# mLSTM and GLA values in one 512-column projection: one pass of the weights over five PSUM banks, ahead of the mLSTM

## The chip, the cores and the metric

The program runs on one NeuronCore of a Trainium2 chip. The metric is the device time of one execution in microseconds (us); lower is better. TensorE (PE) does the matmuls, VectorE (DVE), ScalarE (ACT) and GpSimd (POOL) the elementwise work, SyncE (SP) issues the DMAs.

## What is computed

Two layers of a diffusion backbone on 640 tokens of width 1024: 128 context tokens (tile 0) and 512 latent tokens (tiles 1 to 4). Cut to what the change touches:

```python
(mq, mk, mv, mo, mg, gq, gk, gv, gg, ga, acq, ackv, akr) = split(h @ w_in)   # one input projection
hf, state = mlstm_scan(q, k, v, gates...)        # v from mv, 4 heads x 64 = 256 columns
hb, state = mlstm_scan(flipped ...)
m_out = head_norm(hf + flip(hb)) * sigmoid(mo)
of, Sf = gla_scan(q, k, v, lg_f, S0)             # v from gv, 4 heads x 64 = 256 columns
ob, Sb = gla_scan(flipped ...)
g_out = head_norm(of + flip(ob)) * silu(gg)
a_out = mla_attention(...)                       # from acq, ackv, akr
out = concat(m_out, g_out, a_out) @ w_out
```

After this mixer each layer has a LayerNorm, a SwiGLU and a second LayerNorm. The four 256-column parts mv, gv, mo and gg have the same input `h` and the same form of product.

## The kernel before

Activations stand transposed in SBUF as `hT`: for each of 8 slices of the model width a 128-row tile, with columns for the tokens (groups of 256 and 384). All large products are made from a high and a low part of each factor, so that one product takes three matmuls (`mm3`, line 62: h·wh, h·wl, l·wh). Weights come by DMA into `raw` (4 buffers) and `wsplit` (line 117) makes the two parts: ACT writes `wh`, DVE or POOL writes `wl` (3 buffers each).

The mixer (line 323) has two ways of projecting. `a_tile` (line 349) holds the weights still and streams tokens, so that its result has features on partitions. `b_tiles` (line 361) holds 128 tokens still and streams 256 columns of weights: for each of the 5 token tiles, 8 slices × 3 matmuls of 128x256 into one PSUM bank `accB`, then an eviction. `b_quarter` (line 377) runs all its tiles. Its four uses in a layer, 120 matmuls each, are:

- quarter 0 (mv), line 406, ahead of the mLSTM, evicted by ACT into `v1`;
- quarter 1 (gv), line 661, in the program text behind the mLSTM and the GLA's q and k projections, evicted by ACT into `gv`;
- quarters 2 (mo) and 3 (gg), lines 704 and 858, which become gates.

The mLSTM (lines 409 to 580) first turns gate rows into scans on DVE (`rowF`, `rowBC`, `rowI`), transposes them on PE (`tokT`), then updates the states `C` position by position (`U` on PE, `kw` and `C` on DVE), and last runs five token tiles, each with `Mb`, `qk` and `hnum` on PE, `Dt` on ACT, POOL and DVE. The GLA first makes gates (`z` on PE; `zb`, `ze` on DVE and ACT) and chunk ends (`ep` and `khT` on PE; `lgl`, `kx`, `qh` on DVE), lines 594 to 634; then state updates (`U2`, shown as `U`, with `S` on DVE) and, for each token tile, `gla_levels`, `gla_scores` and `gla_rows` (lines 731 to 808: `Xq` on DVE, `Xk` on POOL, `lv`, `lw` and `go` on PE). In layer 0 the conditioning weights are used beside all this: `ada` (line 168) loads 1 MB at a time into the one buffer `araw4` and multiplies it by 4 matmuls; `weave(n)` advances it by n such steps.

Order of the work: the text above is the program order only. A scheduler sets each engine's order by readiness and program order, so independent projections fill PE between dependent steps. Engines take their own instructions strictly in that order. PSUM has 8 banks: in the mixer ring `a` has 2, `q` 2, and `b` 3 in layer 0 (with 1 for `ada`) or 4 in layer 1.

Of the kernel before, what the change touches and what calls it, by code (L numbers as in the profile page):

```python
# [6 lines left out]
F32 = mybir.dt.float32  # L7
F32R = mybir.dt.float32r
AF = mybir.ActivationFunctionType
# [5 lines left out]
L = 2  # L15
D = 1024
NT = 5
# [14 lines left out]
def tcol(t):  # L32
    return (0, t * 128) if t < 2 else (1, (t - 2) * 128)


def build(nc, tc, I, O, dbg=None, layers=L, stop=None):
    V, S, P, T = nc.vector, nc.scalar, nc.gpsimd, nc.tensor
# [7 lines left out]
    def act(out, in_, f, **kw):  # L45
        return S.activation(out=out, in_=in_, func=f, **kw)  # L46
# [70 lines left out]
    def wsplit(src, n=1024, own=None, e=V):  # L117
        r = raw()
        dma(r[:, :n] if len(src.shape) == 2 else
            r[:, :n].rearrange("p (a b) -> p a b", a=src.shape[1]), src)  # L120
        p, tag, bufs = own or (wp, "w", SPL)
        h = p.tile([128, 1024], F32R, tag=tag + "h", bufs=bufs, name="wh")
        l = p.tile([128, 1024], F32R, tag=tag + "l", bufs=bufs, name="wl")
        act(h[:, :n], r[:, :n], AF.Copy)
        tt(l[:, :n], r[:, :n], h[:, :n].bitcast(F32), SUB, e=e)
        return h, l
# [196 lines left out]
    def mixer(l, hT, adas, pm0, ws=None):  # L323
# [11 lines left out]
        g0 = g0s.enter_context(pool(f"glas{l}"))  # L335
# [25 lines left out]
        def b_tiles(q, evac, wv=0):  # L361
            ws = []
            for u in range(2):
                weave(wv)
                ws.append(wsplit(I["w_inB"][l, q, u]))
            for t in range(NT):
                g, o = tcol(t)
                h, lo = hT[g]
                acc = pa("accB")
                for k in range(8):  # L370
                    wh, wl = ws[k // 4]
                    c = slice((k % 4) * 256, (k % 4) * 256 + 256)
                    mm3(acc[:, :256], (h[:, k, o:o + 128], lo[:, k, o:o + 128]), (wh[:, c], wl[:, c]), k == 0, k == 7)
                evac(acc[:, :256], t)
                yield

        def b_quarter(q, evac, wv=0):
            for _ in b_tiles(q, evac, wv):
                pass
# [5 lines left out]
        v1 = mp.tile([128, NT, 4, 65], F32, name="v1")  # L385
# [7 lines left out]
        else:  # L393
            todo = [(g, f) for g in range(2) for f in first]
            for part in (todo[:5], todo[5:]):
                accs = [pt("aabbb"[i], "acc") for i in range(len(part))]
                for kk in range(4):
                    for acc, (g, ((src, M), (wh, wl), dst)) in zip(accs, part):
                        h, lo = hT[g]
                        for k in range(2 * kk, 2 * kk + 2):  # L400
                            c = slice(k * M, k * M + M)
# [1 line left out]
                for acc, (g, ((src, M), w, dst)) in zip(accs, part):  # L403
                    act(dst[:, GO[g]:GO[g] + GN[g]], acc[:M, :GN[g]], AF.Copy)

        b_quarter(0, lambda acc, t: act(v1[:, t, :, 0:64], acc.rearrange("p (h v) -> p h v", h=4), AF.Copy))


        R = [64, NT, 128]
# [34 lines left out]
        mo = mp.tile([64, NT], F32, name="mo")  # L444
# [60 lines left out]
        for j in range(0, 4):  # L505
            for d in range(2):
                t = pos2tile(d, j)
# [18 lines left out]
        for t in range(NT):  # L526
            c = slice(t * 128, (t + 1) * 128)
# [53 lines left out]
        m1.close()  # L581


        gv = g0.tile([128, NT, 256], F32, name="gv")
        qh = [pp.tile([128, 2, 128], F32, name=f"qh{t}") for t in range(NT)]
        kh = [pp.tile([128, 2, 128], F32, name=f"kh{t}") for t in range(NT)]
        zb = [g0.tile([128, 256], F32, name=f"zb{t}") for t in range(NT)]
# [70 lines left out]
        a_tile(I["w_inA"][l, 6], 128, evs(kg), wv=3)  # L658
        for t in ORD:
            gla_gates(t)  # L660
        b_quarter(1, lambda acc, t: act(gv[:, t, :], acc, AF.Copy), wv=3)
        kxs = {}
        for i, t in enumerate(ORD):
            kxs[i] = gla_ends(t)
# [771 lines left out]
def layout(x):  # L1436
    f = np.float32
    o = _consts()
    o["xp"] = x["x_prompt"].reshape(128, D)
    o["xs"] = x["x_sample"].reshape(512, D)  # L1440
    o["cT"] = np.stack([x["c_ctx"].reshape(8, 128).T, x["c"].reshape(8, 128).T], 2)
    o["w_ada"], o["b_ada"] = x["w_ada"], x["b_ada"]
    w = x["w_in"]
    sp = np.cumsum((128, 128, 256, 256, 16, 128, 128, 256, 256, 32, 256, 128, 32))[:-1]
    mq, mk, mv, mo, mg, gq, gk, gv, gg, ga, acq, ackv, akr = np.split(w, sp, axis=2)
    sw = np.concatenate([np.arange(8, 16), np.arange(0, 8), np.arange(24, 32), np.arange(16, 24)])

    def mt(a):
        return a.reshape(L, 8, 128, a.shape[2]).transpose(0, 2, 1, 3).reshape(L, 128, -1)
    o["w_inA"] = np.stack([mt(a) for a in (acq[..., :128], acq[..., 128:], ackv, mq, mk, gq, gk)], 1)  # L1450
    o["w_inM"] = mt(np.concatenate([akr, akr[..., sw], ga, mg], 2))

    def halves(a):
        n = a.shape[1] // 256
        return a.reshape(L, n, 2, 128, 2, 512).transpose(0, 4, 1, 3, 2, 5).reshape(L, 2, n, 128, 1024)
    o["w_inB"] = np.stack([a.reshape(L, 2, 4, 128, 256).transpose(0, 1, 3, 2, 4).reshape(L, 2, 128, 1024)
                           for a in (mv, gv, mo, gg)], 1)
    gb = np.zeros((L, 64, 2), f)
    b = x["m_gate_b"]
    gb[:, 0:4, 0], gb[:, 0:4, 1] = b[:, 0:4], b[:, 4:8]  # L1460
    gb[:, 32:36, 0], gb[:, 32:36, 1] = b[:, 8:12], b[:, 12:16]
    o["gbias"] = gb
    o["gn"] = np.concatenate([x["m_norm_g"], x["g_norm_g"]], 1)
    w2 = np.zeros((L, 32, 256), f)
    w2[:, 0:16, 0:128] = x["g_w2"][:, 0]
    w2[:, 16:32, 128:256] = x["g_w2"][:, 1]
    o["g_w2"] = w2
    o["g_b2"] = x["g_b2"].reshape(L, 256)
    o["agn"] = np.stack([x["a_q_norm_g"][:, :128], x["a_q_norm_g"][:, 128:], x["a_kv_norm_g"]], 2)
    uq = x["a_w_uq"].reshape(L, 2, 128, 8, 96)  # L1470
    nope, rope = uq[..., :64].reshape(L, 2, 128, 512), uq[..., 64:]
    o["w_uq"] = np.concatenate([nope, rope.reshape(L, 2, 128, 256), rope[..., sw].reshape(L, 2, 128, 256)], 3)
    ukv = x["a_w_ukv"].reshape(L, 128, 8, 128)
    o["w_ukv"] = np.concatenate([ukv[..., :64].reshape(L, 128, 512), ukv[..., 64:].reshape(L, 128, 512)], 2)
    o["ckvT"] = x["cache_mla_ckv"][0].transpose(0, 2, 1)
    o["krT"] = x["cache_mla_krope"][0].transpose(0, 2, 1)
    o["w_out"] = halves(x["w_out"])
    ln = np.stack([x["ln1_g"], x["ln1_b"], x["ln2_g"], x["ln2_b"]], 1)
    o["ln_rows"] = ln
    o["ln_fm"] = ln.reshape(L, 4, 8, 128).transpose(0, 3, 1, 2)  # L1480
    for n in ("gate", "up"):
        o["w_" + n] = x["w_ffn_" + n].reshape(L, 8, 128, NM, 128).transpose(0, 3, 2, 1, 4).reshape(L, NM, 128, 1024)
    o["w_down"] = x["w_ffn_down"].reshape(L, NM, 128, 2, 512).transpose(0, 3, 1, 2, 4)
    ci = np.zeros((L, 2, 4, 32, 4, 65), f)
    si = np.zeros((L, 2, 4, 32, 4, 64), f)
    for h in range(4):
        ci[:, :, h, :, h, :64] = x["state_mlstm_C"][0][:, :, h]
        ci[:, :, h, :, h, 64] = x["state_mlstm_n"][0][:, :, h]
        si[:, :, h, :, h] = x["state_gla_S"][0][:, :, h]
    o["cinit"] = ci.reshape(L, 2, 128, 260)  # L1490
    o["sinit"] = si.reshape(L, 2, 128, 256)
    m0 = np.zeros((L, 64, 1), f)
    m0[:, 0:4, 0] = x["state_mlstm_m"][0][:, 0]
    m0[:, 32:36, 0] = x["state_mlstm_m"][0][:, 1]
    o["m0"] = m0
    return {k: np.ascontiguousarray(v) for k, v in o.items()}
# [29 lines left out]
```

## Time and profile before

| what | value |
|---|---|
| three runs | 1853.81, 1857.25, 1860.08 us (median 1857.25) |
| the profiled execution | 1855.06 us, of which its span is 1853.3 us |
| mean granted TensorE clock | 0.968 of full speed |
| busy share of the span | PE 94%, PE weight loads 83%, DVE 58%, ACT 37%, POOL 19% |
| layer 0 mixer, from the first `accB` to the first `racc` (attention's q) | 60.6 to 285.9 us |
| layer 1 mixer, the same stretch | 992.8 to 1187.9 us |

Matmuls overlap in the pipeline: the duration of one is longer than the step to the next, so costs are taken from start to start. A granted clock of 1.00 in a stretch is 2.4 GHz, 0.50 is 1.2 GHz.

### The profile page before, as it was taken

Reading aid. Unit: us, or ns where it says so; the run is one execution under the profiler, and the core shown is the slowest. Engines: PE = TensorE matmul, PEld = TensorE weight load, DVE = VectorE, ACT = ScalarE, POOL = GpSimd, SP = SyncE. Lnnn points to the kernel's source line nnn. Section 1 sums busy time; section 2 is a strip of 40 time slices with the busy share of each in tenths; the row PEclk is TensorE's granted clock in tenths of the full one; section 3 lists DMA queues with packets and bytes.
Section 4 is the critical chain, followed back from the end, with each engine's and each line's share of the span. In section 5 each row is a group of like instructions: output and inputs, shape, how many; then the busy total and the mean of one; then the engine's idle time right before and its main releaser. Section 6 shows DMA issues by size and latency. Waiting matters only on the chain.

```text
span 1853.3 us, 28755 instructions
## 1 busy us (share of the span) xinstructions
PE 1745.0 (94%) x11360; PEld 1535.3 (83%) x11360; DVE 1072.2 (58%) x1996; ACT 685.2 (37%) x1418; POOL 343.7 (19%) x286
## 2 busy tenths in 40 slices
PE   7989888989999999999989999899999999999996
PEld 4867777768999899899868887776789989989995
DVE  3545588646588757564476667776475234233237
ACT  4335357643422122122243455576262212222221
POOL 0011435321330000000031136334026000000003
PEclk9989999999999999999998899899999999999998
DMA  9654322023246445342223223211412222213211
GB/s 317 231 141 163 111 59 62 18 107 114 93 159 207 139 138 163 117 130 93 79 80 120 25 67 90 59 24 39 170 69 85 75 80 72 77 58 92 79 58 57
DMA packets 82678, 190.70 MB, mean 103 GB/s; under 512 B 12712, under 2 KB 28360, under 8 KB 80496
## 3 DMA queue, kind: packets, MB, share of 16 engines
q1 hardware_dynamic: 82544, 188.87, 32.6%
q8 instruction: 89, 1.46, 0.3%
q14 instruction: 45, 0.37, 0.1%
HBM read 174.00 MB, written 5.70 MB: 97 GB/s over the span
## 4 chain that ended last, share of the span: by engine, by line
PE 78%; DVE 11%; ACT 4%; DMA 3%; issue 2%; POOL 2%; SPq 0%; DVEq 0%; ACTq 0%; POOLq 0%
PE accd L60 21%; PE pu L60 16%; PE pg L60 16%; PE acc L60 6%; PE accB L60 5%; PE sp L60 2%; PE O L60 2%; PE ada L60 2%; DMA araw<-w_ada 2%; POOL x L49 1%; PE PT L1010 1%; PE hnum L60 1%; PE racc L60 1%; ACT Pt L46 1%; DVE Xq L49 1%
## 5 line engine op out<-in xcount | busy, mean ns | idle before, releaser
L46 ACT ACTIVATE wh<-raw 128x1024 fp32r<-128x1024 f32 (+2 forms) x193 | 197.5, 1027 | 551.4 <-PE accd L60 230.3
L49 DVE TENSOR_TENSOR wl<-raw,wh 128x1024 fp32r<-128x1024 f32 (+2 forms) x169 | 214.2, 1270 | 305.7 <-ACT wh L46 305.3
L60 PE MATMUL pg<-l,wh 128*128 128x256 f32 (+1 forms) x704 | 219.9, 312 | 8.6 <-DVE l L49 8.6
L60 PE MATMUL pu<-h,wl 128*128 128x256 f32 (+1 forms) x704 | 217.9, 310 | 1.9 <-POOL wl L49 1.9
L60 PE MATMUL pg<-h,wh 128*128 128x256 f32 (+1 forms) x704 | 219.1, 311 | 0.0
L60 PE MATMUL pg<-h,wl 128*128 128x384 f32 (+1 forms) x704 | 218.9, 311 | 0.0
L60 PE MATMUL pu<-l,wh 128*128 128x256 f32 (+1 forms) x704 | 218.1, 310 | 0.0
L60 PE MATMUL pu<-h,wh 128*128 128x256 f32 (+1 forms) x704 | 218.0, 310 | 0.0
L49 POOL TENSOR_TENSOR x<-x,lrow 128x512 f32<-128x512 f32 (+1 forms) x22 | 42.1, 1933 | 826.3 <-PE hTt L281 415.0
L60 PE MATMUL accd<-wl,gh 128*128 128x512 f32 x440 | 173.1, 394 | 0.0
L60 PE MATMUL accd<-wh,gh 128*128 128x512 f32 x440 | 171.6, 393 | 0.0
L60 PE MATMUL accd<-wh,gl 128*128 128x512 f32 x440 | 170.7, 390 | 0.0
L60 PEld LDWEIGHTS pg<-l,wh 128*128 128x128 f32 x704 | 134.6, 191 | 10.4 <-DVE l L49 9.0
L60 PEld LDWEIGHTS pu<-h,wl 128*128 128x128 f32 x704 | 134.2, 191 | 2.3 <-POOL wl L49 2.3
L60 PEld LDWEIGHTS pg<-h,wh 128*128 128x128 f32 x704 | 134.5, 191 | 1.4 <-issue 1.2
L60 PEld LDWEIGHTS pg<-h,wl 128*128 128x128 f32 x704 | 134.5, 191 | 1.1 <-issue 1.0
L60 PEld LDWEIGHTS pu<-l,wh 128*128 128x128 f32 x704 | 134.4, 191 | 0.0
L60 PEld LDWEIGHTS pu<-h,wh 128*128 128x128 f32 x704 | 134.1, 190 | 0.0
L57 DVE SCALAR_TENSOR_TENSOR aacc<-araw,scT,aacc 128x512 f32<-128x512 f32 x168 | 117.9, 745 | 12.4 <-DMA araw<-w_ada 12.3
L49 DVE TENSOR_TENSOR sg<-sg,pu 128x256 f32<-128x256 f32 (+1 forms) x88 | 42.7, 485 | 121.4 <-PE pu L60 121.2
L60 PE MATMUL accB<-wh,h 128*128 128x256 f32 x320 | 99.5, 311 | 3.0 <-DVE S L57 2.4
L60 PEld LDWEIGHTS accd<-wh,gh 128*128 128x128 f32 x440 | 82.6, 188 | 19.2 <-issue 0.6
(357 smaller groups left out, 3756.4 us busy)
## 6 DMA issues: line engine op xcount, KB each, us to landing
araw<-w_ada SPq DMA_DIRECT2D x128, 256.0 KB
raw<-w_gate SPq DMA_DIRECT2D x44, 512.0 KB
raw<-w_up SPq DMA_DIRECT2D x44, 512.0 KB
raw<-w_down SPq DMA_DIRECT2D x40, 512.0 KB
araw<-w_ada SPq DMA_DIRECT2D x16, 1024.0 KB
raw<-w_inB SPq DMA_DIRECT2D x16, 512.0 KB
raw<-w_out SPq DMA_DIRECT2D x16, 512.0 KB
raw<-w_inA SPq DMA_DIRECT2D x12, 512.0 KB
```

The costliest lines, as they stand in the source:

```text
L46: return S.activation(out=out, in_=in_, func=f, **kw)
L49: return e.tensor_tensor(out=out, in0=a, in1=b, op=op)
L57: return e.scalar_tensor_tensor(out=out, in0=a, scalar=s, in1=b, op0=o0, op1=o1)
L60: return T.matmul(out, lhsT, rhs, start=start, stop=stop)
L1010: T.transpose(tr[:, (t - 1) * 128:t * 128], Ps[h, t][:, kt * 128:(kt + 1) * 128], ident)
```

## The change

Quarters 0 and 1 become one projection `b_values`, at the place of quarter 0. It has four weight units of 2 slices × 512 columns (mv and gv side by side, array `w_inV`), and five accumulators `accV` at once, one for each token tile, in the 2 banks of ring `a` and 3 of ring `b`. Each unit is loaded, split and passed over all five tiles; after the fourth unit each tile is evicted, its first half by ACT into `v1`, its second by DVE into `gv`. At the old place of quarter 1 stays one `weave(6)` in place of two `weave(3)`. Quarters 2 and 3 are as before.

```diff
@@ b_tiles
-                ws.append(wsplit(I["w_inB"][l, q, u]))
+                ws.append(wsplit(I["w_inB"][l, q - 2, u]))
@@ new
+        def b_values(evac):
+            accs = [pt("aabbb"[t], "accV") for t in range(NT)]
+            for u in range(4):
+                wh, wl = wsplit(I["w_inV"][l, u])
+                for t in range(NT):
+                    g, o = tcol(t)
+                    h, lo = hT[g]
+                    for i in range(2):
+                        k = 2 * u + i
+                        c = slice(512 * i, 512 * i + 512)
+                        mm3(accs[t], (h[:, k, o:o + 128], lo[:, k, o:o + 128]), (wh[:, c], wl[:, c]), k == 0, k == 7)
+            for t in range(NT):
+                evac(accs[t], t)
@@ ahead of the mLSTM
-        b_quarter(0, lambda acc, t: act(v1[:, t, :, 0:64], acc.rearrange("p (h v) -> p h v", h=4), AF.Copy))
+        gv = g0.tile([128, NT, 256], F32, name="gv")
+
+        def ev_values(acc, t):
+            act(v1[:, t, :, 0:64], acc[:, 0:256].rearrange("p (h v) -> p h v", h=4), AF.Copy)
+            V.tensor_copy(gv[:, t, :], acc[:, 256:512])
+        b_values(ev_values)
@@ GLA, behind the mLSTM
-        gv = g0.tile([128, NT, 256], F32, name="gv")
...
-        b_quarter(1, lambda acc, t: act(gv[:, t, :], acc, AF.Copy), wv=3)
+        weave(6)
```

The scheduler puts the instructions of both mixers in another order. Two places show it. The first is PE's order in layer 1 behind the mLSTM's state updates (`U`), where its first token tiles begin. Before:

```order
L60 MATMUL U<-v_9581,kw 32x65 x8
L60 MATMUL z<-gw_9574,misc 128x256 x2
L60 MATMUL U<-v_9581,kw 32x65 x4
L60 MATMUL Mb<-rowM,ident 128x128 x8
L60 MATMUL z<-gw_9574,misc 128x256 x2
L60 MATMUL accB<-wh,h_89 128x256
L60 MATMUL accB<-wl,h_89 128x256
L60 MATMUL accB<-wh,l_90 128x256
```

and at the same place of the change:

```order
L60 MATMUL U<-v_9456,kw 32x65 x8
L60 MATMUL Mb<-rowM,ident 128x128 x8
L60 MATMUL z<-gw_9449,misc 128x256 x2
L60 MATMUL ep<-wseg,lgh 128x256
L60 MATMUL ep<-wseg,lgl 128x256
L60 MATMUL ep<-wseg,lgh 128x256
L60 MATMUL ep<-wseg,lgl 128x256
L60 MATMUL hnum<-v_9456,Dt 128x65 x2
L60 MATMUL ep<-wseg,lgh 128x256
L656 MATMUL khT<-ident,kx 128x128 x2
L60 MATMUL qk<-qm,km 128x128 x2
L60 MATMUL hnum<-v_9456,Dt 128x65 x2
```

Where 120 matmuls of quarter 1 lay between the mLSTM's tiles, the GLA's chunk ends (`ep`, `khT`) now follow at once, and `acc` matmuls of the attention's latents, which stood behind the mLSTM, come after them as filling. The second place is PE's order in layer 0 around the same `U`, with the steps of `ada`. Before:

```order
L60 MATMUL U<-v_455,kw 32x65 x4
L60 MATMUL ada<-araw,scT 32x512 x4
L60 MATMUL U<-v_455,kw 32x65 x4
L60 MATMUL z<-gw_448,misc 128x256 x2
L60 MATMUL U<-v_455,kw 32x65 x8
L60 MATMUL z<-gw_448,misc 128x256 x2
L60 MATMUL ada<-araw,scT 32x512 x4
L60 MATMUL U<-v_455,kw 32x65 x8
L60 MATMUL Mb<-rowM,ident 128x128 x4
L60 MATMUL accB<-wh,h_89 128x256
```

and in the change:

```order
L60 MATMUL ada<-araw,scT 32x512 x4
L60 MATMUL z<-gw_448,misc 128x256 x2
L60 MATMUL U<-v_455,kw 32x65 x8
L60 MATMUL Mb<-rowM,ident 128x128 x4
L60 MATMUL z<-gw_448,misc 128x256
L60 MATMUL ep<-wseg,lgh 128x256
L60 MATMUL Mb<-rowM,ident 128x128 x4
L60 MATMUL ada<-araw,scT 32x512 x4
L60 MATMUL ep<-wseg,lgl 128x256
L60 MATMUL ep<-wseg,lgh 128x256
```

The pair of `ada` steps with little between them, which lay inside the `U` before, now lies around the last `U`, and the next steps follow among `ep` and `Mb` instead of among `accB`. Outside the two mixers PE's order is the same as before.

## Rows read from the trace of the kernel before

**Rows 1.** Page, part 1: busy us (share of the span) and instructions.
```profile
PE 1745.0 (94%) x11360; PEld 1535.3 (83%) x11360; DVE 1072.2 (58%) x1996; ACT 685.2 (37%) x1418; POOL 343.7 (19%) x286
```
**Rows 2.** Page, part 4: the chain that ended last, by engine.
```profile
PE 78%; DVE 11%; ACT 4%; DMA 3%; issue 2%; POOL 2%; SPq 0%; DVEq 0%; ACTq 0%; POOLq 0%
```
**Rows 3.** PE groups by form: busy us, mean ns | idle before.
```profile
L60 PE MATMUL accd<-wl,gh 128*128 128x512 f32 x440 | 173.1, 394 | 0.0
...
L60 PE MATMUL accB<-wh,h 128*128 128x256 f32 x320 | 99.5, 311 | 3.0 <-DVE S L57 2.4 <-DVE zb L49 0.6
```
**Rows 4.** Timeline, PE, layer 1: start us, us; quarter 0's first and last matmul.
```profile
992.77 0.28 PE L60 MATMUL accB<-wh,h 128*128 128x256 f32 x1
...
1007.03 0.28 PE L60 MATMUL accB<-wh,l 128*128 128x256 f32 x1
```
**Rows 5.** Timeline, PE, layer 0's w_out: first and last of 27 consecutive 512-column matmuls.
```profile
451.29 0.39 PE L60 MATMUL accd<-wh,l 128*128 128x512 f32 x1
...
457.28 0.40 PE L60 MATMUL accd<-wl,h 128*128 128x512 f32 x1
```
**Rows 6.** Tile accB: evictions, duration ns min/median/max.
```profile
L46 ACT ACTIVATE v<-accB x10: 361/384/385, 65.3 to 1009.1; 128x256 f32<-128x256 f32 x10
...
L646 DVE COPY graw<-accB x10: 404/414/426, 268.5 to 1191.8; 128x256 f32<-128x256 f32 x10
```
**Rows 7.** Page, part 5: the weight splits on ACT and DVE.
```profile
L46 ACT ACTIVATE wh<-raw 128x1024 fp32r<-128x1024 f32 (+2 forms) x193 | 197.5, 1027 | 551.4 <-PE accd L60 230.3
L49 DVE TENSOR_TENSOR wl<-raw,wh 128x1024 fp32r<-128x1024 f32 (+2 forms) x169 | 214.2, 1270 | 305.7 <-ACT wh L46 305.3
```
**Rows 8.** Windows, layer 1's mixer: us, busy PE, PEld, DVE, ACT, POOL; clock; DMA.
```profile
992.80:1021.00 28.20, 28.20 (x222) 25.80 (x221) 17.96 (x32) 11.24 (x25) 0.00 (x0) 1.00 0.34 111
1021.00:1040.00 19.00, 15.97 (x129) 12.50 (x128) 15.45 (x43) 7.94 (x22) 2.84 (x2) 0.85 0.59 60
1040.00:1070.00 30.00, 30.00 (x238) 27.74 (x238) 15.27 (x38) 15.08 (x42) 6.42 (x5) 0.92 0.00 1
1070.00:1090.00 20.00, 17.61 (x113) 14.52 (x113) 17.66 (x51) 13.07 (x42) 3.98 (x3) 0.91 0.15 54
...
1121.50:1187.90 66.40, 61.13 (x668) 51.14 (x659) 53.78 (x139) 34.63 (x98) 27.87 (x44) 0.95 0.20 52
```
**Rows 9.** Timeline, PE, layer 1, behind U: [idle before <-releaser].
```profile
1035.13 2.07 PE L60 MATMUL z<-gw,misc 32*128 32x256 f32 x4 [1.88 <-DVE zb L49]
1037.83 0.58 PE L60 MATMUL accB<-wh,h 128*128 128x256 f32 x1 [0.63 <-DVE zb L49]
```
**Rows 10.** Timeline, PE, layer 0: steps of ada.
```profile
101.70 1.06 PE L60 MATMUL ada<-araw,scT 128*32 128x512 f32 x8 [0.29 <-DMA araw<-w_ada]
...
113.94 1.94 PE L60 MATMUL ada<-araw,scT 128*32 128x512 f32 x8 [5.32 <-DMA araw<-w_ada]
...
165.08 1.06 PE L60 MATMUL ada<-araw,scT 128*32 128x512 f32 x8 [0.59 <-DMA araw<-w_ada]
```
**Rows 11.** Timeline, SP's queue, layer 0: issues.
```profile
100.69 0.43 SPq L40 DMA_DIRECT2D o_n<-Cout  x1
102.83 0.34 SPq L40 DMA_DIRECT2D araw<-w_ada  x1
...
158.00 0.33 SPq L40 DMA_DIRECT2D araw<-w_ada  x1
```
**Rows 12.** Windows, layer 0's mixer, columns as in rows 8.
```profile
108.60:113.90 5.30, 0.02 (x1) 0.00 (x0) 3.51 (x12) 2.00 (x5) 0.00 (x0) 0.50 0.73 233
113.90:123.80 9.90, 9.86 (x62) 7.81 (x63) 5.49 (x14) 2.99 (x9) 1.29 (x1) 0.54 0.34 119
...
213.90:285.90 72.00, 63.89 (x669) 54.68 (x670) 55.06 (x145) 37.13 (x103) 30.38 (x48) 0.91 0.21 52
```
**Rows 13.** Timeline, PE, layer 0, GLA: two waits.
```profile
213.88 0.93 PE L60 MATMUL lv<-Xqe,Xk 128*32 128x128 f32 x25 [2.58 <-DMA Xqe<-Xq]
...
255.51 0.32 PE L828 MATMUL Rb<-ident,rr 128*128 128x128 f32 x1 [3.95 <-DVE acq L57]
```

More of the change, by code (lines that the diff above doesn't have):

```diff
@@ L375, in b_tiles, with b_quarter @@
                 yield
+        def b_quarter(q, evac, wv=0):
+            for _ in b_tiles(q, evac, wv):
+                pass
+        def b_values(evac):
[11 more added lines that the diff above has]
+                evac(accs[t], t)
         def b_quarter(q, evac, wv=0):
@@ L1456, in layout @@
     o["w_inB"] = np.stack([a.reshape(L, 2, 4, 128, 256).transpose(0, 1, 3, 2, 4).reshape(L, 2, 128, 1024)
-                           for a in (mv, gv, mo, gg)], 1)
+                           for a in (mo, gg)], 1)
+    o["w_inV"] = (np.concatenate([mv, gv], 2).reshape(L, 4, 2, 128, 512).transpose(0, 1, 3, 2, 4)
+                  .reshape(L, 4, 128, 1024))
     gb = np.zeros((L, 64, 2), f)
```

## The prediction

> **What bounds the kernel now.** I read the page first: PE is busy 94% of the span [rows 1] and holds 78% of the chain that ended last, DVE 11% [rows 2]. So what shortens PE's queue counts, where PE is the engine that everything waits for. Outside the two mixers PE's order doesn't change, so the question is only what the mixers do, each some 200 us long. The windows of layer 1's mixer [rows 8] show that it isn't one bound but a sequence. From 992.8 to 1021.0 PE is busy all 28.20 us and DVE 17.96 us. From 1021 to 1040 (state updates `U`, `C`, GLA gates) PE stands idle 19.00 - 15.97 = 3.03 us while DVE works 15.45 us, and the timeline names it: PE waits for DVE's `zb` [rows 9]. From 1040 to 1070 PE is full again with quarter 1's `accB` between the mLSTM's tiles, and DVE only half busy. From 1070 to 1090 (chunk ends `ep`, `khT`) DVE is busy 17.66 of 20 us and PE loses 2.39 us. From 1121.5 to 1187.9 (GLA tiles) DVE has 53.78 of 66.40 us, PE loses 5.27 us. Layer 0 is alike, with one worse place: PE stands 5.32 us for a 1 MB load of `ada` [rows 10], and the clock is then granted at 0.54 for 9.90 us [rows 12].
>
> **The change part by part.**
>
> *The products.* Removed are, in two layers, 2 × 2 × 120 = 480 matmuls of 256 columns, half of the `accB` groups (one of three groups of 320 is shown in [rows 3]); added are 2 × 120 = 240 of 512. Durations overlap, so I take steps: 120 `accB` matmuls go from 992.77 to 1007.03 [rows 4], 119 steps of 0.1198 us; 27 of the 512-column `accd` from 451.29 to 457.28 [rows 5], 26 steps of 0.2304 us. 480 × 0.1198 = 57.5 us go, 240 × 0.2304 = 55.3 us come: 2.2 us less. The same columns are streamed; only the fixed part of a matmul is saved, 2 × 0.1198 - 0.2304 = 0.0092 us for each of 240.
> The Trainium skill (TensorE: Matmul & The Clock Gate, section "Wait — 56ns, not 53.3ns?") puts the fixed part at about 2.5 ns a matmul. By it the saving would be 240 × 0.0025 = 0.6 us; the steps here, 9.2 ns, disagree, and I keep them. Either is under what can be measured.
>
> *Weight loads and splits.* Weight loads into PE halve for these products, but they are already hidden: the 256-column matmuls run at 0.1198 us, near the rate of the wide ones per column. Bytes and splits stay the same, four units of 512 KB for a layer. A unit now serves 30 matmuls, 6.9 us, and a split takes 1.03 us on ACT and 1.27 us on DVE [rows 7], so the next is ready in time; cost nothing. If a unit came late, PE would have only `qk` to do, since five banks are taken; that is a rival.
>
> *Evictions.* Ten `gv` copies move from ACT (0.384 us) to DVE (0.414 us) [rows 6]: 10 × 0.41 = 4.1 us of DVE for both layers, at a point where DVE's scans are done and PE has the `acc` of the GLA's q and k before it. Hidden; without that cover 2 us a layer.
>
> *What moves.* The projection ahead of the mLSTM lasts 27.7 us instead of 14.3 us, so the mLSTM starts some 13.4 us later in each layer. In return 120 matmuls leave the space between its tiles. If PE stays full this is an exchange and costs nothing, and the order shows what fills instead: 3 × 48 `acc` matmuls of the latents, pulled forward from behind the mLSTM. The scans' DVE chain, which ran beside 14.3 us of `accB`, now lies wholly beside `accV`; it had not held up PE before either, so this gains nothing.
>
> *The two DVE-heavy pieces meet.* The gates and state updates (15.45 us of DVE) and the chunk ends (17.66 us), 30 us apart before [rows 8], now follow one another: together 33.1 us of DVE against 33.6 us of PE in 39 us. Best, the pockets keep their 3.03 + 2.39 = 5.4 us of PE idle or lose it; worst, without `accB` between them the idle doubles, 5.4 us more a layer, since the mLSTM's own `Dt`, `hr` and `hs` now queue on DVE between `lgl`, `kx` and `qh`. I take zero, since PE work and DVE work are even and the old pockets had just this mix.
>
> *The `ada` steps of layer 0.* Each step needs a load that is issued only when the step before has read the single buffer. After 101.70 the load was issued at 102.83, behind the small `o_n` stores [rows 11], and was used at 113.94: 12.24 us from step to step. Another, issued at 158.00, was used at 165.08 after a short wait [rows 10, 11]: 7.1 us from issue. The new order again has one step behind those stores and then a close pair. Bounds: the 5.32 us wait and the slow clock after it vanish (5.32 + 9.90 × 0.46 = 9.9 us gained, if the load lands under other work), or a second such wait comes (5.3 us). I take zero, as the same stores still stand ahead of the same load. SP's queue is otherwise passed by nothing: the `w_inV` loads take the places of `w_inB` and `w_inA`.
>
> *The GLA tiles.* Quarter 2 now runs beside the state updates `U2` ahead of the tiles, quarter 3 between them; before, both were between them and the rest came as a tail. The tiles are as heavy on DVE as on PE, so less PE work there does not shorten them much. At best the idle falls by half: layer 0 lost 72.00 - 63.89 = 8.1 us, layer 1 5.3 us [rows 8, 12], and two of the waits are 2.58 and 3.95 us [rows 13]. I take zero here too.
>
> *Sum.* -2.2 us. The profiled execution took 1855.06 us, so 1852.9 by that; it stands 2.2 us under the median of 1857.25, against which the forecast is **1855 us**.
>
> **The rivals.** What a measurement of this kernel can tell from no change is about 0.3%, 5.6 us: from 1851.7 to 1862.8 is "same".
>
> *Faster: the GLA tiles close up.* With `U2` and its `S` updates done beforehand, DVE has less in the tiles. For it: DVE is the fuller engine there. Against: PE has less to fill with, and the mLSTM ends later, so the tiles start later. Price: half of 13.4 us of idle, 6.7 us, with the 2.2 us: 1857.25 - 8.9 = 1848 us. With layer 0's `ada` wait gone as well it would be 1839 us, which needs both.
>
> *Slower: DVE and the `ada` loads hold PE behind `U`.* The place is the first two mLSTM tiles, where the order has `ep`, `khT`, `hnum` and no free-standing matmuls. It decides as soon as DVE needs longer for its 33 us than PE for its own; every microsecond then stops PE. Price: 5.4 us a layer, one more `ada` wait of 5.3 us, less 2.2 us: 1857.25 + 13.9 = 1871 us in full; for half of it, which I find likelier, 1863 to 1866 us. For it: DVE waits already show there [rows 9]. Against: PE's own work is as long.
>
> *The change does not do what it says:* the one pass stalls at its units, because all five banks are held and `wl` stands in DVE's queue between the scans. One split of 2.3 us exposed at each of 8 units gives 18 us, 1873 us. Against it stand the 6.9 us for each unit.
>
> **How the numbers follow.** The exchange without net effect has 0.49, the closed-up tiles 0.29, the held PE 0.19, the stalled pass 0.03. So faster by over 0.3%: 0.29, within 0.3%: 0.49, slower: 0.22. The range from 1845 to 1866 takes in the faster case at its price and some more, and the slower one at half its price; the full prices, about 2 in 10, stay outside.
>
> **What would show it.** Right: `accV` steps of 0.23 us in a block of some 28 us without idle; in layer 1 two DVE-full pockets merged behind `U` with about 5 us of PE idle; the first `racc` of each layer within 3 us of where it stood from the first value matmul (225.3 and 195.1 us). The forecast is wrong if that distance changes by more, and the windows between the first value matmul, the last `hnum`, the first `lv` and the first `racc` tell where: in the mLSTM (held PE), before the tiles (`ada`), or in the tiles (closed up).

## The result, and the profile after

The changed kernel is slower: median 1874.24 us of 9 runs (1865.07 to 1890.21) against 1853.81 us of 9 runs of the kernel before (1844.13 to 1866.01). The ratio is 1.0111, 95% interval 1.0078 to 1.0144. The profiled execution took 1881.65 us, span 1879.9 us, 26.6 us more than before's span.

In the totals of the page hardly anything moves (part 1 of the page; the chain of part 4 by engine; compare [rows 1, 2]):

```profile
PE 1760.0 (94%) x11120; PEld 1534.4 (82%) x11120; DVE 1085.8 (58%) x2006; ACT 682.5 (36%) x1408; POOL 338.8 (18%) x286
PE 78%; DVE 11%; ACT 4%; DMA 3%; issue 2%; POOL 2%; SPq 1%; DVEq 0%; ACTq 0%; POOLq 0%
```

PE has 240 matmuls fewer and is busy 15 us longer. What moves is TensorE's clock, 0.968 on average before and now (cores view):

```profile
core 0: 1879.9 us, clock 0.956
```

Span times clock, roughly the time at full clock, is 1794 us before and 1797 us after: 3 of the 26.6 us. The windows of layer 1's mixer say where the clock is lost (columns as in [rows 8]; the seventh number, behind POOL, is the clock):

```profile
1010.00:1036.00 26.00, 26.00 (x116) 21.49 (x115) 17.94 (x29) 8.67 (x14) 0.00 (x0) 1.00 0.42 138
...
1060.00:1070.00 10.00, 5.80 (x41) 3.99 (x41) 9.43 (x28) 5.21 (x17) 1.11 (x1) 0.57 0.32 84
1070.00:1080.00 10.00, 9.06 (x46) 7.78 (x48) 5.75 (x16) 5.64 (x19) 1.94 (x3) 0.50 0.00 0
1080.00:1090.00 10.00, 10.00 (x44) 8.24 (x45) 7.40 (x22) 5.26 (x17) 3.43 (x3) 0.50 0.00 1
1090.00:1100.00 10.00, 9.45 (x61) 7.32 (x60) 7.01 (x24) 6.32 (x21) 1.26 (x1) 0.84 0.01 2
1100.00:1110.00 10.00, 9.40 (x43) 9.00 (x44) 4.34 (x11) 3.42 (x11) 2.56 (x2) 0.54 0.00 0
1110.00:1120.00 10.00, 10.00 (x77) 9.00 (x76) 3.35 (x8) 5.64 (x15) 1.29 (x1) 1.00 0.06 7
```

PE waits behind `U` from 1060 to 1070, and the clock falls to 0.50 (1.2 GHz). It stays there to 1092, is up for 7 us and is down again from 1099 to 1109, although PE is listed as busy for 37.9 of the 40 us from 1070 to 1110. Before, the same stretch had `accB` between the tiles and a clock of 0.92 [rows 8, third row]. Layer 0, the same view:

```profile
110.00:117.60 7.60, 6.69 (x77) 4.32 (x77) 3.85 (x16) 1.44 (x2) 0.00 (x0) 1.00 0.90 71
117.60:125.40 7.80, 0.01 (x3) 0.02 (x3) 5.17 (x16) 1.89 (x5) 0.00 (x0) 0.61 0.65 173
125.40:140.00 14.60, 14.07 (x67) 8.59 (x68) 9.95 (x26) 6.37 (x20) 2.54 (x2) 0.50 0.39 130
140.00:150.00 10.00, 10.00 (x45) 6.99 (x44) 3.48 (x13) 4.63 (x15) 1.36 (x1) 0.50 0.19 52
...
160.00:170.00 10.00, 10.00 (x45) 8.89 (x46) 3.52 (x11) 1.73 (x6) 1.29 (x1) 0.50 0.41 134
170.00:180.00 10.00, 10.00 (x69) 8.08 (x69) 5.58 (x13) 4.79 (x14) 1.32 (x2) 0.97 0.32 105
```

Here the low stretch lasts 51 us (0.50 from 119.4 to 170.4); before, it was 17 us (106 to 123 us; the windows of [rows 12] cut off its start). It ends shortly behind the first of the latents' `acc` products, at 166.40 us. PE at 10.00 of 10 us with 45 matmuls and PE at 10.00 with 69 look alike in the busy column. The groups by form show the same products at either clock, from 140 to 160 us and then from 180 to 215 us (busy, mean ns):

```profile
L60 PE MATMUL Mb<-rowM,ident 32*128 32x128 f32 x24 | 6.1, 429 | 0.0
L60 PE MATMUL hnum<-v,Dt 128*128 128x65 f32 x16 | 4.0, 419 | 0.0
...
L60 PE MATMUL hnum<-v,Dt 128*128 128x65 f32 x40 | 5.7, 278 | 0.0
L60 PE MATMUL Mb<-rowM,ident 32*128 32x128 f32 x24 | 3.7, 287 | 0.0
```

The waits in front of the low stretches (timeline of PE; layer 0, then layer 1):

```profile
110.16 1.04 PE L60 MATMUL ada<-araw,scT 128*32 128x512 f32 x8
125.39 1.94 PE L60 MATMUL ada<-araw,scT 128*32 128x512 f32 x8 [7.80 <-DMA araw<-w_ada]
...
1062.61 0.66 PE L60 MATMUL U<-v,kw 128*32 128x65 f32 x16 [1.57 <-DVE kw L49]
1069.12 0.55 PE L60 MATMUL ep<-wseg,lgh 128*128 128x256 f32 x1 [2.30 <-ACT ze L46]
1070.50 0.58 PE L60 MATMUL ep<-wseg,lgl 128*128 128x256 f32 x1 [0.83 <-DVE lgl L49]
```

I kept one ledger for all kernels. It runs from the first `U` of a layer to the first `accd` (the output projection), in windows of about 3 us: idle is length less PE's busy time, lost clock is busy time × (1 - clock), and the rest is PE's work at full clock. "To U" is the time from the first value product to the first `U`. Each cell gives layer 0 / layer 1 in us, from one profiled execution each.

| kernel | to U | U to accd | idle | lost clock | rest |
|---|---|---|---|---|---|
| before | 37.3 / 27.6 | 308.1 / 287.9 | 33.3 / 25.1 | 15.9 / 14.5 | 258.8 / 248.4 |
| after | 48.5 / 40.2 | 314.3 / 284.5 | 39.0 / 31.8 | 30.0 / 22.2 | 245.3 / 230.4 |
| after, again | 48.5 / 40.2 | 307.1 / 282.5 | 38.9 / 28.7 | 20.8 / 23.1 | 247.3 / 230.6 |
| move alone | 47.8 / 39.3 | 307.4 / 277.6 | 31.5 / 27.4 | 22.4 / 17.9 | 253.5 / 232.3 |
| move alone, again | 44.8 / 39.3 | 319.0 / 284.4 | 31.2 / 28.0 | 35.3 / 24.7 | 252.5 / 231.7 |
| after + filler | 48.5 / 40.2 | 311.7 / 287.1 | 33.5 / 24.3 | 18.8 / 16.4 | 259.4 / 246.4 |
| before - quarter 1 | 37.2 / 27.6 | 303.4 / 276.4 | 38.4 / 26.0 | 18.5 / 20.0 | 246.5 / 230.5 |
| after, early set-up | 33.4 / 30.7 | 308.5 / 301.9 | 35.2 / 28.1 | 9.6 / 33.3 | 263.7 / 240.5 |
| after, latents first | 48.5 / 40.2 | 311.5 / 277.0 | 40.9 / 31.5 | 23.0 / 14.0 | 247.6 / 231.4 |
| after, early set-up, latents first | 33.4 / 30.7 | 322.5 / 285.4 | 38.3 / 29.9 | 19.4 / 13.9 | 264.8 / 241.6 |

For the change: `U` comes 11.2 + 12.6 = 23.8 us later. Behind it 13.5 + 18.0 us of PE's work are gone, but idle rose by 12.4 us and lost clock by 21.8 us, so that this stretch is 6.2 us longer in layer 0 and only 3.4 us shorter in layer 1. 23.8 + 6.2 - 3.4 = 26.6 us, the whole difference of the two spans. This is one execution, and 7 us above the median; in the other profile of the change idle is 9.2 us and lost clock 13.5 us above the kernel before.

The two losses lie in different places. Windows from the first `U` to the last `hnum` (the mLSTM) and from there to the first `lv` (the GLA's tiles), first layer 0, then layer 1; before:

```profile
97.98:183.73 85.75, 77.64 (x576) 59.50 (x576) 47.48 (x134) 36.97 (x104) 14.60 (x10) 0.90 0.48 145
183.73:213.88 30.15, 27.26 (x197) 23.88 (x196) 13.66 (x41) 11.88 (x26) 12.75 (x14) 1.00 0.56 173
1020.32:1096.41 76.09, 70.67 (x536) 61.37 (x535) 49.42 (x133) 38.10 (x108) 13.24 (x10) 0.91 0.19 30
1096.41:1121.49 25.08, 24.91 (x179) 24.23 (x182) 14.31 (x40) 12.80 (x31) 17.18 (x19) 0.93 0.51 148
```

and in the change:

```profile
109.91:209.71 99.80, 90.57 (x541) 67.08 (x541) 48.43 (x135) 37.29 (x104) 13.19 (x10) 0.74 0.41 118
209.71:252.75 43.04, 35.24 (x290) 30.15 (x290) 26.96 (x69) 15.32 (x38) 19.91 (x22) 0.92 0.44 143
1049.89:1130.07 80.18, 73.73 (x477) 63.53 (x476) 49.15 (x134) 38.62 (x107) 12.88 (x10) 0.74 0.11 22
1130.07:1155.24 25.17, 19.96 (x172) 18.32 (x174) 15.78 (x40) 10.23 (x27) 14.60 (x15) 0.97 0.40 116
```

In the mLSTM the clock falls from 0.90 and 0.91 to 0.74, while PE's idle time there (length less busy) grows by only 1.1 and 1.0 us. Most of the added idle lies behind it, ahead of the GLA's tiles: 7.8 instead of 2.9 us, and 5.2 instead of 0.2 us.

### The profile page after: what moved, and what is told of

It is laid out like the page before. It is cut to its first block, busy times and chain, and to the rows that moved or that the text cites. A ratio compares the mean times of both kernels' runs of the same rounds, so it can differ in the third digit from the quotient of the medians.

```text
span 1879.9 us, 28284 instructions
## 1 busy us (share of the span) xinstructions
PE 1760.0 (94%) x11120; PEld 1534.4 (82%) x11120; DVE 1085.8 (58%) x2006; ACT 682.5 (36%) x1408; POOL 338.8 (18%) x286
## 4 chain that ended last, share of the span: by engine, by line
PE 78%; DVE 11%; ACT 4%; DMA 3%; issue 2%; POOL 2%; SPq 1%; DVEq 0%; ACTq 0%; POOLq 0%
PE accd L60 20%; PE pu L60 16%; PE pg L60 15%; PE acc L60 7%; PE accV L60 3%; PE sp L60 2%; PE O L60 2%; PE ada L60 2%; PE hnum L60 2%; PE accB L60 2%; POOL x L49 1%; PE PT L1033 1%; PE Mb L60 1%; DMA araw<-w_ada 1%; PE ep L60 1%
## 5 line engine op out<-in xcount | busy, mean ns | idle before, releaser
L60 PEld LDWEIGHTS accd<-wh,gl 128*128 128x128 f32 x440 | 82.7, 188 | 18.5
```

The costliest lines, as they stand in the source:

```text
L60: return T.matmul(out, lhsT, rhs, start=start, stop=stop)
```

## The experiments

Theory A: quarter 1's dense products were what kept the clock up and filled the waits behind `U`. The rivals: B, the one-pass form; C, VectorE; D, the `ada` load behind the small stores in layer 0.

### The move without the form, and the form without the move

Move alone (kernel before; 256 columns, two units each, one bank for a tile):

```diff
         b_quarter(0, ...)
+        gv = g0.tile([128, NT, 256], F32, name="gv")
+        b_quarter(1, lambda acc, t: act(gv[:, t, :], acc, AF.Copy))
...
-        b_quarter(1, lambda acc, t: act(gv[:, t, :], acc, AF.Copy), wv=3)
+        weave(6)
```

> The kernel before with only the move: the mLSTM's values and the GLA's values are two separate products 256 columns wide, two units each, one bank for a token tile, and both stand ahead of the mLSTM; nothing is passed once over five banks. Theory A (with quarter 1 gone from between the mLSTM's tiles, TensorE has only small fp32 products there, its clock is granted at 0.5 and stays there): the loss of the change comes in full, 1870 to 1880 us, ratio to the kernel before 1.009 to 1.015, and in layer 1 the granted clock is about 0.5 for some 40 us behind the updates U. Rival B (the wide one-pass form with its five held banks costs the time): within 5 us of the kernel before, ratio 0.997 to 1.003.

Form alone (kernel before; quarter 1 stays):

```diff
-        b_quarter(0, ...)
+        accs = [pt("aabbb"[t], "accV") for t in range(NT)]
+        for u in range(2):
+            wh, wl = wsplit(I["w_inB"][l, 0, u])
...
+        for t in range(NT):
+            act(v1[:, t, :, 0:64], accs[t][:, 0:256]..., AF.Copy)
```

> The kernel before with only the form: the mLSTM's values alone, 256 columns wide, are passed once over five PSUM banks with the tiles evicted at the end; quarter 1 stays between the mLSTM's tiles. Theory A: as the kernel before, ratio 0.997 to 1.003, since the dense products stay where they were and the clock with them. Rival B (the form costs it): a good part of the change's 20 us, ratio 1.005 to 1.013.

Measured: move alone 1862.7 us, ratio 1.0058 (1.0035 to 1.0080); form alone 1854.7 us, 1.0023 (0.9991 to 1.0056). The move is slower by itself, but by about 11 us, half of what A expected. The form alone is within what can be told from no change, though its interval reaches 1.0056.

The change and the move alone were run once more, side by side:

> The changed kernel once more, beside the move alone, for what is left between them. If the one-pass form has a price of its own, the changed kernel stays 5 to 12 us above the move alone, here about 1870 to 1876 us; if the difference was only the spread of the clock between executions, the two agree within 4 us.

> The move alone once more: 1860 to 1866 us if the form has a price (the one pass keeps the five banks, so the kg and qg products fill the time ahead of U instead of standing behind it: 37 and 50 of those 96 left behind the first U, against 60 and 60 here); 1866 to 1874 us if the difference was chance.

Measured: 1875.7 us, 1.0103 (1.0073 to 1.0133), and 1869.3 us, 1.0065 (1.0035 to 1.0094). They stay 6.4 us apart, with overlapping intervals. The mean clock over these runs is 0.9663 before, 0.9600 for the change and 0.9595 for the move; span times clock is 1793, 1798 and 1792 us. So all that the move loses is clock; the change has some 5 us besides. In the ledger they stand as idle time: against the move, `U` comes 2 to 5 us later in the change, idle behind it is 8 to 12 us more, and PE's work there 6 to 10 us less. Part of that work is `kg` and `qg`: of their 96 products the change leaves 17 behind the first `U` in layer 0 (not 37, as the expectation has it) and 50 in layer 1, the move 60 and 60.

The two profiles of the move alone show most clearly that the clock sets this time. It is the same program. Windows of layer 0, first execution:

```profile
130.00:150.00 20.00, 19.71 (x95) 13.45 (x94) 14.38 (x41) 12.63 (x41) 3.81 (x3) 0.59 0.39 131
150.00:170.00 20.00, 20.00 (x150) 15.10 (x148) 12.81 (x37) 10.55 (x34) 5.17 (x4) 1.00 0.43 132
```

and second:

```profile
130.00:150.00 20.00, 19.71 (x78) 14.70 (x74) 12.93 (x40) 11.24 (x36) 3.36 (x4) 0.50 0.40 132
150.00:170.00 20.00, 20.00 (x93) 14.82 (x91) 9.28 (x27) 7.46 (x23) 3.60 (x3) 0.53 0.30 102
```

PE goes through the same products in the same order (`Mb`, `hnum`, `ep`, `qk`, steps of `ada`, towards the end the first `acc`) and is busy all 20 us; at full clock it does 150 matmuls, at 0.53 it does 93. The second span is 1876.1 us, the first 1860.4 us. Lost clock behind `U` is 12.9 + 6.8 = 19.7 us more in the second; an earlier `U` makes good 3.0 us. Over the ten later runs of the move the span goes from 1861.7 to 1878.1 us as the mean clock goes from 0.963 to 0.953, and span times clock stays between 1790 and 1795 us.

### Dense products put back

Added work, in the changed kernel: quarter 2's products once more, thrown away.

```diff
-        weave(6)
+        junk = g0.tile([128, 128], F32, name="junk")
+        b_quarter(2, lambda acc, t: act(junk, acc[:, 0:128], AF.Copy), wv=3)
```

> The changed kernel with quarter 2's products (120 of 256 columns a layer, with their two units of weights) computed once more where quarter 1 used to stand, and thrown away: 2 x 14.4 us of dense work at full clock is added. Theory A: the filler keeps the clock up, so most of the added work is paid for by the small products that now run at full speed: 1866 to 1882 us, within 8 us of the changed kernel. Rival C or D (VectorE, or the loads, set the length of the stretch): the filler lies in idle time, at best the time of the changed kernel, but with the clock still low; if PE is the bound with its clock not mattering, 1874 + 28.8 = 1903 us.

Measured: 1877.1 us, 1.0151 (1.0098 to 1.0203): 2.9 us above the changed kernel by the medians, 7 us by the two ratios, for 28.8 us of added work. The ledger gives idle and lost clock as in the kernel before. Layer 1 behind `U` (windows):

```profile
1057.70:1067.70 10.00, 6.41 (x52) 4.75 (x45) 9.42 (x28) 5.08 (x16) 1.58 (x2) 0.60 0.32 80
1067.70:1077.70 10.00, 10.00 (x83) 9.37 (x82) 5.01 (x12) 5.20 (x17) 1.55 (x2) 0.89 0.00 0
1077.70:1087.70 10.00, 10.00 (x82) 9.13 (x80) 5.40 (x13) 3.85 (x13) 3.44 (x3) 1.00 0.01 2
```

The clock falls at the same wait and is back within 10 us, once dense products follow. (Behind layer 1's output projection this one execution, 1894.9 us, is some 15 us longer than the others; that part isn't used.)

Taken away, in the kernel before: quarter 1 is left out (the GLA's values are zeros). And doubled: quarter 1 is computed twice.

```diff
-        b_quarter(1, lambda acc, t: act(gv[:, t, :], acc, AF.Copy), wv=3)
+        weave(6)
+        P.memset(gv, 0.0)
```

> The kernel before with quarter 1 (the GLA's values) left out: 2 x 120 products of 256 columns and their units of weights are gone, the GLA's values are zeros. 28.8 us of TensorE's work at full clock is taken out, all of it behind U, where the change takes it away too; nothing is added ahead of U. Theory A (behind U those products only filled waits and kept the clock up, so taking them away saves next to nothing, and the change's price is simply what it adds ahead of U): 1846 to 1858 us, ratio 0.996 to 1.003. Rival E (an even exchange, as predicted; the change loses its time in another way): about 1825 us, ratio 0.985.

> The kernel before with quarter 1's products computed twice in their place behind U: 28.8 us of work added where the change takes it away. Theory A: the waits and the slow clock there are mostly filled already by the first copy (10.9 us idle and 10.4 us lost clock were left from U to the residual in layer 1), so more than half of it is paid: 1866 to 1880 us, ratio 1.007 to 1.014. If the filler were never free, 1880 to 1884 us; if it were still free, 1850 to 1858 us.

Measured: left out, 1840.0 us, 0.9904 (0.9862 to 0.9945), which is 16 us saved of 28.8; doubled, 1877.4 us, 1.0108 (1.0054 to 1.0161), which is 21.5 us paid of 28.8. So neither extreme holds: behind `U` taking dense work away returns about half of it, and a second helping is mostly paid. Without quarter 1 the kernel before shows the same low stretch in layer 1 (windows):

```profile
1025.00:1035.00 10.00, 5.47 (x41) 3.38 (x41) 9.52 (x24) 6.04 (x18) 2.81 (x2) 0.72 0.37 84
1035.00:1045.00 10.00, 9.44 (x48) 8.10 (x48) 4.84 (x16) 5.54 (x19) 0.82 (x1) 0.50 0.00 0
1045.00:1055.00 10.00, 10.00 (x44) 8.28 (x42) 7.83 (x23) 5.13 (x16) 2.98 (x3) 0.50 0.00 0
```

In layer 0 it does not: there the clock is 0.50 for 17 us (107.9 to 124.9), as in the kernel before, so that the missing quarter alone doesn't keep it down.

The two halves of the move nearly add up: were 28.8 us paid ahead of `U` in full and 16 us got back behind it, 12.8 us would be left, near the 11 and 12 us of the move's two ratios. But the ledger has `U` only 19 to 22 us later in the move, so this agreement is in part luck.

### The latents' products as filler

No work is added: the three latents' products are written ahead of all chunk ends, or one by one between the first three.

```diff
+        for i in range(3):
+            a_tile(I["w_inA"][l, i], 128, evlat(i))
         kxs = {}
         for i, t in enumerate(ORD):
             kxs[i] = gla_ends(t)
...
-        for i in range(3):
-            a_tile(I["w_inA"][l, i], 128, evlat(i), wv=3)
...
```

> The changed kernel with the three latents' products (3 x 48 dense products a layer) written ahead of the GLA's chunk ends, so that they come between the mLSTM's first tiles, where quarter 1 was; no work is added. Theory A: the clock stays up behind U and most of the loss comes back, 1850 to 1862 us, ratio to the kernel before 0.996 to 1.005. Rival C (the mixers are as long because the chunk ends and the mLSTM's tiles both need VectorE; the order of products does not matter): some of it back as well, since the chunk ends come later, but the clock would stay at 0.5 in the first tiles. Rival D (the load of ada behind the small stores in layer 0): no more than layer 1's part back, 1865 us or more.

> The changed kernel with the three latents' products (3 x 48 a layer, no work added) written one by one between the first GLA chunk ends instead of behind all of them. When they all stood ahead of the ends, the clock was up in the first tiles and fell instead behind them, where the ends met the last mLSTM tiles alone. Theory A: spread out they serve both places; idle plus lost clock from U to the residual falls, 1856 to 1866 us, under the version with all of them first (1868). Rival C (VectorE sets the length of that stretch, whatever lies between): as that version, 1866 to 1872 us.

Measured: ahead 1868.1 us, 1.0087 (1.0048 to 1.0126); between 1874.7 us, 1.0116 (1.0085 to 1.0148). Both expectations of A were too good; the first time is one that rival D allowed (1865 us or more), the second lies above both ranges. With the latents first, layer 1's clock is up in the first tiles and falls to 0.50 only from 1122 to 1132, where the chunk ends now meet the last tiles; its lost clock, 14.0 us, is that of the kernel before. In layer 0 the clock still falls behind the wait for `ada`. And idle behind `U` stays 14 us above the kernel before (72.4 against 58.4 us): so not all of the loss is clock; waits were left.

### VectorE, and the load of `ada`

The multiplications of the chunk ends on GpSimd, in the changed kernel:

```diff
-            tt(kx, kx, kg[:, c]...to_broadcast([128, 2, 128]), MUL)
+            tt(kx, kx, kg[:, c]...to_broadcast([128, 2, 128]), MUL, e=P)
```

and the same for `qh`.

> The changed kernel with the two multiplications of each GLA chunk end (the products of kx and of qh) on GpSimd, which is nearly idle there, instead of VectorE: 20 multiplications leave VectorE's queue in that stretch, and PE's products stay in nearly the same order. Rival C (VectorE's two pieces, the gates with the updates and the ends with the mLSTM's tiles, hold PE): 5 us a layer or more come back, 1860 to 1866 us. Theory A (PE is busy all the time there, at 0.5 of its clock): little changes, 1868 to 1880 us, and the clock is low for as long.

Measured: 1882.4 us, 1.0157 (1.0124 to 1.0190), above both ranges. Nothing came back, which speaks against rival C: less on DVE, and the clock is low all the same (windows, layer 1). The test isn't clean, though, as the product of `kx` takes 0.75 us on GpSimd and 0.42 us on DVE.

```profile
1071.00:1081.00 10.00, 9.67 (x47) 7.77 (x46) 4.49 (x18) 6.34 (x20) 2.98 (x3) 0.50 0.00 0
1081.00:1091.00 10.00, 10.00 (x48) 8.73 (x47) 4.58 (x12) 4.09 (x14) 5.00 (x6) 0.53 0.01 2
```

The small stores of C and n behind the mLSTM, in the changed kernel and in the kernel before:

```diff
-                if j == 0:
-                    dma(O["C"][l, d]..., Cout[:, d, 0:64])
-                    dma(O["n"][l, d]..., Cout[:, d, 64:65])
...
+        zz = mp.tile([128, 1], F32, name="zz")
+        ts(zz, mean[:, 0:1], 0.0, None, MUL, e=P)
+        Cst = mp.tile([128, 2, 65], F32, name="Cst")
+        act(Cst, Cout, AF.Identity, bias=zz)
+        for d in range(2):
+            dma(O["C"][l, d]..., Cst[:, d, 0:64])
+            dma(O["n"][l, d]..., Cst[:, d, 64:65])
         m1.close()
```

> The changed kernel with the stores of C and n of the mLSTM (small rows, which stood in SyncE's queue just ahead of a 1 MB load of ada) made from a copy that waits for the last mLSTM tile, so that they leave behind the mLSTM; 2 small instructions a layer are added. Theory A, refined (after any wait behind U the clock is at 0.5 and the small products that follow keep it there): the 7.8 us wait of layer 0 falls to under 3 us and the stretch at 0.5 begins later, but it is still there for 30 us or more: 1864 to 1872 us, 2 to 10 us under the changed kernel. Rival D (the load behind the small stores is the cause in layer 0, the slow clock its consequence): layer 0's part of the loss goes, clock 1.00 soon behind U, 1855 to 1863 us.

> The kernel before with the same late stores. In it PE stood 5.32 us for that load and the clock was at about 0.5 for 10 us behind it. If the stores delay the load, 5 to 10 us are gained, 1844 to 1850 us, ratio 0.995 to 0.998; if the load is as slow without them, 1.000 +- 0.002.

Measured: 1878.6 us, 1.0134 (1.0102 to 1.0166), above both ranges, and 1851.3 us, 0.9992 (0.9976 to 1.0009), without the 5 to 10 us that a delayed load had been worth. The stores do delay the load: with them it is issued at 112.41 us and used at 125.39, without them issued at 111.51 and used at 116.51, and the wait of layer 0 in the changed kernel falls from 7.80 to 0.71 us.

```profile
116.51 1.06 PE L60 MATMUL ada<-araw,scT 128*32 128x512 f32 x8 [0.71 <-DMA araw<-w_ada]
124.61 1.94 PE L60 MATMUL ada<-araw,scT 128*32 128x512 f32 x8
```

But the next `ada` step is at 1.94 us again, the slow clock: it falls behind the next waits, of 0.58 and 1.99 us. Rival D had a real wait and a wrong cause; taking the wait away brought no time.

### The set-up of the mLSTM under the values

With five banks held, `tokT` starts only behind `accV` (27.3 us after its first product in layer 1; 15.9 us in the move alone). So the set-up (`kT`, `tokT`, `dps`, `ip`) was put on the two `q` banks and written ahead of the values, in the changed kernel and in the kernel before.

> The changed kernel with the mLSTM's set-up (the transposes kT and tokT, dps, ip) on the two banks of q, which the one pass does not hold, kT made first, and all of it written ahead of the values, so that it runs under accV; U can follow accV at once and the 96 dense products of kg and qg stay behind it. Theory F (with the five banks held the set-up starts only behind accV, 12.9 us in layer 1 from tokT to U, and kg and qg are spent as its cover): U comes 28 to 32 us behind the first accV product instead of 48.5 and 40.2, and with the dense products behind U the clock falls for less long: 1852 to 1864 us. Rival G (the changed kernel's distance from the move alone is the clock's chance spread): U comes earlier, but the stretch behind it is as much longer, 1868 to 1878 us.

> The kernel before with the same early set-up. There the set-up already ran under quarter 0's products and behind them (U 27.6 us behind the first product in layer 1), so U can come at most some 8 us earlier and the same dense products lie behind it: 1845 to 1856 us, ratio 0.994 to 1.002. Were the start of U all that counts, 16 us would be gained, 1836 to 1840 us.

Measured: 1870.9 us, 1.0097 (1.0074 to 1.0120), and 1852.1 us, 0.9985 (0.9971 to 0.9999). `U` came at 33.4 and 30.7 us as wanted, and yet the time stayed: theory F's 1852 to 1864 us was wrong, and the time is one that rival G expected. Layer 0 kept its clock up; layer 1 lost 33.3 us of clock, more than any other (windows of layer 1):

```profile
1017.00:1037.00 20.00, 20.00 (x182) 16.37 (x181) 12.85 (x38) 6.43 (x17) 0.00 (x0) 1.00 0.56 57
1037.00:1057.00 20.00, 19.11 (x92) 15.05 (x92) 14.76 (x37) 13.09 (x36) 5.94 (x5) 0.64 0.09 26
1057.00:1077.00 20.00, 20.00 (x86) 16.87 (x84) 10.70 (x34) 10.35 (x33) 3.35 (x3) 0.50 0.01 2
```

From 1037 to 1057 PE is idle for 0.89 us in all, and the clock falls there too; from 1042.6 to 1086.8 PE is then never idle and the clock is 0.50. Here an earlier start of the mLSTM was worth little.

Two combinations followed: the early set-up with the latents ahead of the ends, and the change with the early set-up in layer 0 alone.

> The changed kernel with the early set-up and the latents' products ahead of the GLA's chunk ends (the edits of two earlier runs together). With the early set-up alone layer 0's clock stayed up and layer 1's was low for some 60 us where the ends and the tiles had no dense products between them. Theory A: with kg, qg and the latents between the tiles that stretch goes and only the ends, now last, are left without dense products: 1850 to 1862 us, ratio 0.998 to 1.005. If the stretch only moves behind the latents, 1862 to 1872 us.

> The change and the early set-up in layer 0 alone (there the ada products, which layer 1 has not, also lie between the tiles); layer 1 as in the kernel before with the early set-up. Theory A: layer 0 was 3.5 us shorter than before at the first product of the output projection, layer 1 is as before: 1845 to 1854 us, ratio 0.994 to 1.000. If layer 0's gain was one execution's clock, 1854 to 1862 us.

Measured: 1870.5 us, 1.0107 (1.0057 to 1.0158), and 1850.1 us, 1.0008 (0.9976 to 1.0040). The first missed A's range again. In the ledger its `U`, PE's work behind it and its lost clock are within 3 us of the kernel before (33.3 against 30.4 us of lost clock), while idle is 9.8 us more (68.2 against 58.4 us); that is most of the 10.9 us between the two spans, and it isn't clock. The second shows that in layer 0, with the early set-up, the change costs nothing that can be told; it gains nothing either.

Last, the kernel before with the early set-up and the late stores:

> The kernel before with the early set-up and the late stores, the two edits whose mean clock was highest: each by itself was within 0.15% of the kernel before (ratios 0.9985 and 0.9992). If what they gain adds up, 1846 to 1852 us, ratio 0.995 to 0.999; if both only remove the same slow stretch behind U in layer 0, 1850 to 1854 us, ratio 0.998 to 1.001.

Measured: 1851.7 us against 1855.9 us, 0.9979 (0.9967 to 0.9991). It is 0.2% under the kernel before; its mean clock is 0.970 against 0.966.

## Why the prediction was wrong

Forecast 1855 us, range 1845 to 1866 us; 1874 us came.

- **The products** were right: the step of `accV` is (1017.88 - 1014.71) / 14 = 0.226 us, the block has no idle time (PE is busy 27.30 of 27.30 us in layer 1), and the saving is 240 × (2 × 0.1198 - 0.2264) = 3.2 us instead of 2.2 us.

```profile
1014.71 0.39 PE L60 MATMUL accV<-wl,h 128*128 128x512 f32 x1
...
1017.88 0.39 PE L60 MATMUL accV<-wh,h 128*128 128x512 f32 x1
```

- **Weight loads, splits, evictions** were right: none of them left PE idle in that block. The rival of the stalled pass did not happen.
- **What moves** is the step that failed: "If PE stays full this is an exchange and costs nothing." 23.8 us came ahead of `U`. Behind it PE's work fell by 31.5 us, but the time grew by 2.8 us, because idle rose by 12.4 us and lost clock by 21.8 us (9.2 and 13.5 us in the other profile). In the mLSTM PE stayed as full as before by the busy column, but at a clock of 0.74 instead of 0.90. The sum took the clock as unchanged, without a reason. The exchange was nearly even only in time at full clock (1794 against 1797 us).
- **The two DVE-heavy pieces meet**: the zero taken was about right for the place that it names. From the first `U` to the last `hnum` idle rose by 1.1 and 1.0 us, far from the worst bound of 5.4 us a layer. The idle that did come, 4.9 and 5.0 us, lies between the last `hnum` and the first `lv`, for which the sum has no term. Not priced at all was the clock behind `U`, 14.1 + 7.7 us, though [rows 12] had such a stretch (0.54 for 9.90 us), which the text used only as a possible gain.
- **The slower rival** (1871 us in full, and half of that thought likelier) had the place and nearly the time, the latter by luck: its reason, DVE and `ada` holding PE idle behind `U`, gave 2 us of idle in the mLSTM, and neither relieving DVE nor taking the `ada` wait away brought time back.
- **The `ada` steps**: 7.80 instead of 5.32 us, 2.5 us where zero was taken. Real, and not what the time hangs on.
- **The GLA tiles** closed up, as the faster rival said: from the first `lv` to the first `racc` 54.1 and 60.8 us instead of 72.1 and 66.4 us. In layer 0 the work that made room was done ahead of them: the stretch between the last `hnum` and the first `lv` grew from 30.1 to 43.0 us.
- **The sign that was named**, the first `racc` within 3 us of its old distance from the first value product, shows the miss: 245.5 and 206.4 us, which is 20.2 and 11.3 us more. To the last `hnum` it is 25.2 and 16.8 us more (11.2 and 12.6 us of it by the later `U`), from there to the first `lv` 12.9 and 0.1 us more, in the tiles 17.9 and 5.6 us less.

Shown are the move's price (11 and 12 us by its two ratios), that the clock in the mLSTM is lower once quarter 1's products are moved away (in the kernel before without them, lower in layer 1 only), that in one and the same program the time follows the clock, and that dense products put back bring both clock and idle to what they were before. Open is why the change has 8 to 12 us more idle time behind `U` than the move alone, and with it the rest of some 6 us between them: the early set-up, made to remove that rest, did not. Open also is why PE's own small products sometimes bring the clock back and sometimes don't: in layer 0 of the move alone it is back at 146.6 us in one execution, with no `acc` product since 127 us, and in the other it is at 0.50 up to 168.7 us, where `acc` products have begun.

## What to carry to other kernels

Before moving independent dense products out of a stretch of small dependent ones, price the small ones at both clocks: what the dense ones hide is not only waits; here the clock was lower without them, too. Read the clock beside the busy share, in windows, since PE at half clock looks fully busy. And where two versions differ by a per cent, compare span times mean clock: here it told the part of the clock (the move alone) from the rest.

## What the hardware showed that I had not expected

The clock can stay at 0.50 with PE busy. In layer 0 of the change it is 0.50 from 119.4 to 170.4 us, and from 140 to 170 PE is busy 30.00 of 30.00 us, while mostly `Mb`, `hnum`, `ep`, `qk` and steps of `ada` run. With the early set-up it is 0.50 from 1042.6 to 1086.8 us with PE busy 44.20 of 44.20 us. How long it lasts differs between two executions of one program: 24 and 51 us on end in layer 0 of the move alone. The Trainium skill (TensorE: Matmul & The Clock Gate, section "What's actually happening") says that the gate follows how busy PE has recently been; the trace agrees as to the fall behind the wait of 7.80 us, but the busy time that a profile lists does not tell here when the clock comes back.

Small stores hold up a large load behind them: the 1 MB load of `ada` behind the stores of C and n made PE wait 7.80 us, and 0.71 us without them, though it was issued only 0.9 us earlier then.
